# Half of the second feed-forward product of an encoder layer by a seven-product block scheme on whole 512-column halves

## The chip, the cores and the metric

The kernel runs on one core of one Trainium2 chip. The metric is the device time of one execution in microseconds (us); less is better. The engines are TensorE (PE in the profile, PEld for its weight loads), VectorE (DVE), ScalarE (ACT), GpSimd (POOL) and SyncE (SP), the last of which here only issues transfers.

## The reference, cut to what matters

One layer of an encoder on `x` of 512 tokens by 1024 features, float32. The change touches the last product and the norm behind it:

```
n2 = rms_norm(h, norm_mlp_pre)                                   # 512 x 1024
hid = square(relu(einsum('bsd,df->bsf', n2, w_up)))              # 512 x 4096
mlp_out = einsum('bsf,fd->bsd', hid, w_down)                     # 512 x 1024, over f = 4096
h = h + rms_norm(mlp_out, norm_mlp_post)
```

## The kernel before, in words

Every large product is made in float32 precision out of three matmuls on rounded halves. An operand `a` is split into `hi` (ScalarE copies it into the type `F32R`, line 79) and `lo` (VectorE subtracts `hi` from `a`, line 80); the helper is `split_into`, and `split_back` (line 888) is the same with its result in a tile of the pool `wback`, tag `hl`, five buffers. `mm3` (lines 82 to 86) then adds `ah*bh + ah*bl + al*bh` into one bank of PSUM: three matmuls, lines 84, 85 and 86.

The order of the instructions on each engine is fixed when the program is built, by the planner of the tile framework: it goes through a modelled time, and among the instructions whose inputs and buffers are there by then, the one written first goes first. `tc.issue_after(ins)` puts what is written in its block behind `ins` on the same engine. A pool with N buffers for a tag hands out the next tile only when an earlier one is no longer read.

The first feed-forward product (`up`, lines 969 to 1003) leaves 32 tiles of `hid`, each 128 features by 512 tokens, in four tiles of eight (`hida` three, `hidb` one). Most of it is already made by a seven-product scheme on 256-column blocks (`product`, line 961).

The second product (`down`, lines 1005 to 1053) sums over those 32 feature tiles f into eight PSUM banks `accs[t][hf]`: t is the block of 128 tokens (0 to 3), hf the half of 512 output columns (0 or 1). The loop over `f2` (line 1018) loads two row blocks of `w_down` at once (1 MB, tile `dnw`, tag `raw`, two buffers, queue of SP, line 1020). For each of the two f it splits the weights (`split_back`, 128x1024) and the hidden tile (`split_into`, 128x512), and calls `down` for the eight banks: 24 matmuls of 128x512 columns for each f, 768 in all. The matmuls of the last four f (`NLAST`) are kept back and done bank by bank, so that the norm behind one block of tokens (`post_norm`, lines 805 to 813) can run beside the matmuls of the next. That norm squares a half on ScalarE with a running sum (line 808), weighs it by the gain on VectorE (line 811), takes the power -0.5 on GpSimd (line 96) and adds the residual on VectorE (line 813); then the block goes out in two transfers (line 1050).

Of the kernel before, what the change touches and what calls it, by code (L numbers as in the profile page):

```python
# [10 lines left out]
F32 = mybir.dt.float32  # L11
F32R = mybir.dt.float32r
AF = mybir.ActivationFunctionType
ALU = mybir.AluOpType
PSUM = bass.MemoryType.PSUM

P = 128
S = 512
D = 1024
KD = D // P  # L20
FF = 4096
KF = FF // P
# [14 lines left out]
def block_kernel(ctx: ExitStack, tc: tile.TileContext, x, norm_mix_pre, w_in, b_gate, ln_v_gain, ln_v_bias,  # L37
                 w_spatial, b_spatial, w_branch_a, w_branch_b, w_out, norm_mix_post, norm_mlp_pre, w_up,
                 w_down, norm_mlp_post, ident_c, rope_c, mask_c, perm_c, out):
    nc = tc.nc  # L40
    x, out, w_in, w_up, w_down, w_out = x[0], out[0], w_in[0], w_up[0], w_down[0], w_out[0]
    w_branch_a, w_branch_b, w_spatial = w_branch_a[0], w_branch_b[0], w_spatial[0]

    def pool(stack, name, bufs=1, space=None, side=None):
        kw = {"side": side} if side else {}
        if space is not None:
            kw["space"] = space
        return stack.enter_context(tc.tile_pool(name=name, bufs=bufs, reuse_waits="tile", **kw))

    consts = pool(ctx, "consts")  # L50
    small = pool(ctx, "small", bufs=4)
# [26 lines left out]
    def split_into(hi, lo, src, sub=nc.vector):  # L78
        nc.scalar.activation(hi, src, AF.Copy)  # L79
        return sub.tensor_tensor(lo, src, hi.bitcast(F32), op=ALU.subtract)  # L80

    def mm3(ps, a, b, start, stop):
        (ah, al), (bh, bl) = a, b
        nc.tensor.matmul(ps, ah, bh, start=start, stop=False)  # L84
        nc.tensor.matmul(ps, ah, bl, start=False, stop=False)  # L85
        return nc.tensor.matmul(ps, al, bh, start=False, stop=stop)  # L86

    def rstd_of(ss, mult, eps=EPS):
        t = small.tile([P, 1], F32, name="rs_in")
        nc.vector.tensor_scalar(t, ss[:, 0:1], mult, eps, op0=ALU.mult, op1=ALU.add)  # L90
        if ss.shape[1] == 2:
            t2 = small.tile([P, 1], F32, name="rs_in2")
            nc.vector.scalar_tensor_tensor(t2, ss[:, 1:2], mult, t, op0=ALU.mult, op1=ALU.add)
            t = t2
        r = small.tile([P, 1], F32, name="rs_out")
        nc.gpsimd.tensor_tensor(r, t, neghalf[:, :1], op=ALU.pow)
        return r
# [6 lines left out]
    right = ExitStack()  # L104
# [20 lines left out]
    start = ExitStack()  # L125
# [91 lines left out]
    for i in range(4):  # L217
        if i + 1 < 4:
            _, hi, lo = norm_x(blocks[i + 1], xts[i + 1], rs[i + 1])
# [4 lines left out]
        b = blocks[i]  # L224
# [4 lines left out]
        t = vtmp.tile([P, 2, GW], F32R, name="v0", bufs=2)  # L229
# [89 lines left out]
    for i, (vec, n) in enumerate(((b_gate, 16), (ln_v_gain, 4), (ln_v_bias, 4), (norm_mlp_pre, 8))):  # L319
        o = (0, 16, 20, 24)[i]  # L320
# [364 lines left out]
    for g2 in range(2):  # L685
        raw = wload([KD, 2 * P], lambda r: [(r, fcols(w_in, COL_U + g2 * 2 * P, KD, 2 * P))], "uw")
        for j in range(2):
            g = 2 * g2 + j
            wh, wl = wsplit(raw[:, :, j * P:(j + 1) * P], sub=nc.gpsimd)
            ps = psA.tile([P, S], F32, name="pf", tag="acc" if g else "T", bufs=4 if g else 1)  # L690
# [14 lines left out]
            t = gpool.tile([P, 4, P], F32, name="sv")  # L705
# [59 lines left out]
    for d in range(GSTD):  # L765
        g2 = gate_rows(d - GSTD)
        raw = gate_raw(d)
        for br in range(2):
            ps = feature_tile(*wsplit(raw[:, :, 1 - br]), KD, nhn, nln)
# [8 lines left out]
    back = ExitStack()  # L778
    psB = pool(back, "psB", space=PSUM)
    spacer(back, 224, "nedge")  # L780
    n2pool = pool(back, "n2pool", bufs=8, side="right")
# [6 lines left out]
    gain = hpool.tile([P, D], F32, name="gain", bufs=1)  # L788
    nc.gpsimd.dma_start(gain, norm_mix_post.to_broadcast([P, D]))
    h2d = tc.dram_tile([S, D], F32, name="h2d")  # L790
    halves = [slice(0, 512), slice(512, 1024)]
# [10 lines left out]
    def all_banks():  # L802
        return [[psB.tile([P, 512], F32, name="pd", tag=tg, bufs=4) for _ in range(2)] for tg in ("tp", "tp", "acc", "acc")]

    def post_norm(pss, gain, ys, dst, res, junk):
        ss = small.tile([P, 2], F32, name="ss2")
        for hf, hs in enumerate(halves):
            nc.scalar.activation(junk[hf], pss[hf].rearrange("p (k c) -> p k c", c=P), AF.Square, accum_out=ss[:, hf:hf + 1])
            if hf:
                r = rstd_of(ss, 1.0 / D)  # L810
            nc.vector.tensor_tensor(ys[hf], pss[hf], gain[:, hs], op=ALU.mult)
        for hf, hs in enumerate(halves):
            nc.vector.scalar_tensor_tensor(dst[:, hs], ys[hf], r, res[:, hs], op0=ALU.mult, op1=ALU.add)
# [38 lines left out]
    for t in range(4):  # L852
# [18 lines left out]
        r = rstd_of(ss, 1.0 / D)  # L871
# [16 lines left out]
    def split_back(src, shape):  # L888
        hl = wback.tile([P, 2] + shape, F32R, name="hl", tag="hl")
        split_into(hl[:, 0], hl[:, 1], src)  # L890
        return hl[:, 0], hl[:, 1]

    hida = pool(back, "hida", bufs=3)
    dn = ExitStack()
    d0pool = pool(dn, "d0pool", bufs=2)
    up = ExitStack()
    upool = pool(up, "upool", bufs=2)
    hid = []
# [1 line left out]
    def hid_of(f):  # L900
        return hid[f // 8][:, f % 8]
# [100 lines left out]
    tail()  # L1002
    up.close()

    dpool = pool(dn, "dpool", bufs=2)
    NLAST = 4
    lpool = pool(dn, "lpool", bufs=1)
    epool = pool(dn, "epool", bufs=NLAST)
    gain = n2pool.tile([P, D], F32, name="gain3", tag="n2")
    nc.gpsimd.dma_start(gain, norm_mlp_post.to_broadcast([P, D]))  # L1010
    accs = all_banks()

    def down(t, f, hf, hh, hl, wh, wl):
        ts_ = slice(t * P, (t + 1) * P)
        mm3(accs[t][hf], (hh[:, ts_], hl[:, ts_]), (wh[:, halves[hf]], wl[:, halves[hf]]), f == 0, f == KF - 1)

    last = []
    for f2 in range(KF // 2):
        raw = wback.tile([P, 2, D], F32, name="dnw", tag="raw", bufs=2)
        nc.sync.dma_start(raw, w_down[f2 * 2 * P:(f2 + 1) * 2 * P].rearrange("(k p) c -> p k c", p=P))  # L1020
        for j in range(2):
            f = 2 * f2 + j
            end = f >= KF - NLAST
            wh, wl = split_back(raw[:, j], [D])
            if end:
                hhl = epool.tile([P, 2, S], F32R, name="hhl")
                hh, hl = hhl[:, 0], hhl[:, 1]
            else:
                dp = dpool if f > 1 else d0pool
                hh = dp.tile([P, S], F32R, name="hh")  # L1030
                hl = dp.tile([P, S], F32R, name="hl")
            with tc.issue_after(late[0].ins), tc.issue_after(late[1].ins):
                split_into(hh, hl, hid_of(f))
            if end:
                last.append((f, hh, hl, wh, wl))
            else:
                for t in range(4):
                    for hf in range(2):
                        down(t, f, hf, hh, hl, wh, wl)
    for t in range(4):  # L1040
        ts_ = slice(t * P, (t + 1) * P)
        h2 = n2pool.tile([P, D], F32, name="h2", tag="n2")
        nc.gpsimd.dma_start(h2, h2d[ts_])
        for hf in range(2):
            for f, hh, hl, wh, wl in last:
                down(t, f, hf, hh, hl, wh, wl)
        o = lpool.tile([P, D], F32, name="o", bufs=2)
        post_norm(accs[t], gain, [lpool.tile([P, 512], F32, name="y", bufs=2) for _ in range(2)], o, h2, [o[:, hs].rearrange("p (k c) -> p k c", c=P) for hs in halves])
        for hs in halves:
            nc.sync.dma_start(out[t * P:(t + 1) * P, hs], o[:, hs])  # L1050
    dn.close()
    back.close()

# [40 lines left out]
```

## Time and profile before

| | us |
|---|---|
| time of the runs: median of 3 (lowest, highest) | 808.02 (807.9, 809.44) |
| span of the profiled execution, first to last instruction | 806.0 |
| its own time | not listed apart from the three runs; the median lies 2.0 above its span |
| PE busy in the span | 793.4 (98%) |
| DVE busy | 540.0 (67%) |
| ACT busy | 422.1 (52%) |
| POOL busy | 59.7 (7%) |

How to read the profile: a row of a group gives the source line (which can be a helper's), the engine, the operation, the tiles written and read with their shapes, the number of instructions, their busy time together and the mean length of one, and then the idle time of the engine in front of them with what ended it. A row of the timeline gives the start, the length, the engine, the line, the operation and the tiles. Matmuls overlap in the pipe, so that the length of one is more than the distance between two; distances between starts are used here.

### The profile page before, as it was taken

The page shows a single profiled execution, that of the slowest core. Times are in us where ns is not written, and L with a number is a line of the kernel's source. Part 1 is how long each engine was busy: PE and PEld are TensorE (multiplying, and loading weights), DVE is VectorE, ACT ScalarE, POOL GpSimd, SP SyncE. Part 2 cuts the span into 40 slices and gives each one's busy share as a digit, 9 for nine tenths or more (in the row PEclk, how much of TensorE's full clock was granted, in tenths as well). Part 3 has the DMA queues.
Part 4 walks back from the last instruction along what each step waited for, and adds up shares of the span by engine and source line. Part 5 has one row for each costly group of instructions (what it writes and reads, how often), then busy time and mean ns, then how long its engine had stood idle before and what let it go on. Part 6 is the DMA issues. An engine that isn't in the chain of part 4 may idle for free.

```text
span 806.0 us, 12336 instructions
## 1 busy us (share of the span) xinstructions
PE 793.4 (98%) x4917; PEld 718.9 (89%) x4917; DVE 540.0 (67%) x915; ACT 422.1 (52%) x721; POOL 59.7 (7%) x86
## 2 busy tenths in 40 slices
PE   9999999999999999999999999999999999999996
PEld 6899999998988889999988899999999888888885
DVE  6784688978655877887655489988896633333324
ACT  6351477878576464554445457666666532332212
POOL 3300100010104300000001102000000000000000
PEclk9999999999999999999999999999999999999999
DMA  9643733343625424353446123333334533332202
GB/s 321 220 119 106 202 94 105 105 132 105 185 74 123 130 79 106 102 134 79 158 159 223 62 79 105 106 106 115 108 114 159 211 105 105 104 105 86 72 1 105
DMA packets 90603, 98.92 MB, mean 123 GB/s; under 512 B 2689, under 2 KB 74401, under 8 KB 90546
## 3 DMA queue, kind: packets, MB, share of 16 engines
q1 hardware_dynamic: 80208, 77.60, 31.5%
q0 software_dynamic: 10336, 20.54, 8.3%
q8 instruction: 38, 0.62, 0.3%
q14 instruction: 19, 0.16, 0.1%
q10 hardware_dynamic: 2, 0.00, 0.0%
HBM read 88.17 MB, written 9.96 MB: 122 GB/s over the span
## 4 chain that ended last, share of the span: by engine, by line
PE 94%; DVE 3%; ACT 2%; issue 0%; DMA 0%; DVEq 0%; POOLq 0%; POOL 0%; ACTq 0%
PE pacc L961 12%; PE pg L343 9%; PE pd L84 9%; PE pd L85 9%; PE pd L86 9%; PE pgacc L343 6%; PE pf L84 5%; PE pf L85 5%; PE pf L86 5%; PE ptp L961 5%; PE pv L85 4%; PE pv L84 4%; PE pv L86 4%; PE pgS L343 2%; PE psb L498 1%; PE py L617 1%
## 5 line engine op out<-in xcount | busy, mean ns | idle before, releaser
L85 PE MATMUL pd<-hl,hh 128*128 128x512 f32 x224 | 87.2, 389 | 0.0
L84 PE MATMUL pd<-hl,hh 128*128 128x512 f32 x224 | 86.5, 389 | 0.0
L86 PE MATMUL pd<-hl 128*128 128x512 f32 x224 | 86.0, 389 | 0.0
L80 DVE TENSOR_TENSOR hl<-hid,hh 128x512 fp32r<-128x512 f32 x28 | 19.2, 693 | 75.6 <-ACT hh L79 75.6
L961 PE MATMUL pacc<-nt,hl 128*128 128x256 f32 x504 | 66.9, 279 | 1.4 <-DVE nt L80 1.4
L79 ACT ACTIVATE hh<-hid 128x512 fp32r<-128x512 f32 x28 | 17.4, 630 | 89.0 <-PE pd L85 89.0
L961 PEld LDWEIGHTS pacc<-nt,hl 128*128 128x128 f32 x504 | 62.3, 188 | 1.6 <-DVE nt L80 1.6
L85 PEld LDWEIGHTS pd<-hl,hh 128*128 128x128 f32 x224 | 42.0, 188 | 8.7
L86 PEld LDWEIGHTS pd<-hl 128*128 128x128 f32 x224 | 42.0, 188 | 8.7
L84 PEld LDWEIGHTS pd<-hl,hh 128*128 128x128 f32 x224 | 42.0, 188 | 8.7
L80 DVE TENSOR_TENSOR hl<-dnw,hl 128x1024 fp32r<-128x1024 f32 x32 | 39.1, 1226 | 14.5 <-ACT hl L79 14.5
L961 PE MATMUL pacc<-n,hl 128*128 128x256 f32 x336 | 44.9, 279 | 0.0
L84 PE MATMUL pf<-nh,hi 128*128 128x512 f32 x112 | 44.6, 398 | 0.0
L74 ACT ACTIVATE hi<-s 128x1024 fp32r<-128x1024 f32 x30 | 31.7, 1059 | 23.9 <-DVE s L330 10.5
L85 PE MATMUL pf<-nl,hi 128*128 128x512 f32 x112 | 43.9, 392 | 0.0
L86 PE MATMUL pf<-nh,lo 128*128 128x512 f32 x112 | 43.9, 392 | 0.0
L79 ACT ACTIVATE hl<-s 128x1024 fp32r<-128x1024 f32 x28 | 29.6, 1057 | 27.1 <-DVE s L945 17.6
L75 DVE TENSOR_TENSOR lo<-s,hi 128x1024 fp32r<-128x1024 f32 x30 | 36.6, 1224 | 9.7 <-ACT hi L74 9.6
L961 PEld LDWEIGHTS pacc<-n,hl 128*128 128x128 f32 x336 | 41.8, 188 | 0.1
L79 ACT ACTIVATE hl<-dnw 128x1024 fp32r<-128x1024 f32 x32 | 33.4, 1048 | 13.1 <-PE pacc L961 7.9
L80 DVE TENSOR_TENSOR hl<-s,hl 128x1024 fp32r<-128x1024 f32 x28 | 34.2, 1221 | 6.6 <-ACT hl L79 6.6
L85 PE MATMUL pv<-lo,nh 128*128 128x512 f32 x96 | 38.2, 397 | 0.0
(361 smaller groups left out, 2227.3 us busy)
## 6 DMA issues: line engine op xcount, KB each, us to landing
upw<-in_w_up_dram SPq DMA_DIRECT2D x16, 1024.0 KB, 5.5
dnw<-in_w_down_dram SPq DMA_DIRECT2D x16, 1024.0 KB, 4.9
qkw<-in_w_in_dram SPq DMA_DIRECT2D x24, 512.0 KB, 5.3
gw<-in_w_in_dram SPq DMA_DIRECT2D x16, 512.0 KB, 5.4
slab<-in_w_in_dram SPq DMA_DIRECT2D x6, 1024.0 KB, 9.4
wow<-in_w_out_dram SPq DMA_DIRECT2D x4, 1024.0 KB, 4.9
w0raw<-in_w_in_dram SPq DMA_DIRECT2D x4, 512.0 KB, 7.0
v0d<-v POOLq DMA_DIRECT2D x4, 512.0 KB, 4.7
```

Source lines behind the costliest of these rows:

```text
L74: nc.scalar.activation(hi, raw, AF.Copy)
L75: (sub or nc.vector).tensor_tensor(lo, raw, hi.bitcast(F32), op=ALU.subtract)
L79: nc.scalar.activation(hi, src, AF.Copy)
L80: return sub.tensor_tensor(lo, src, hi.bitcast(F32), op=ALU.subtract)
L84: nc.tensor.matmul(ps, ah, bh, start=start, stop=False)
L85: nc.tensor.matmul(ps, ah, bl, start=False, stop=False)
L86: return nc.tensor.matmul(ps, al, bh, start=False, stop=stop)
L343: nc.tensor.matmul(ps, a[:, j], b[:, j], start=first and not (j or i), stop=(j == KH - 1 and i == 2), skip_group_check=True)
L498: nc.tensor.matmul(ps[:, rr, g - 1], got["q", g][:, r], got["k", g][:, r], start=True, stop=True)
L617: nc.tensor.matmul(o, v12[:, g, r], ptb[r // 2][:, r % 2, g], start=False, stop=(r == 3 and g == 1), skip_group_check=True)
L961: nc.tensor.matmul(ps, a[:, j], b[:, j], start=first and not (j or m), stop=(j == KH - 1 and m == 2), skip_group_check=True)
```

## The change

Of the 32 feature tiles, f = 0 to 15 stay as they were (`plain`, two f at a time, f2 = 0 to 7). The other sixteen are taken as a 2x2 block product: the hidden operand A in blocks of tokens (rows 0 to 255 and 256 to 511) by the parity of f, the weights B in blocks of the parity of f by the column half. Each block of B is eight row blocks of 128 by 512 columns, handled in two chunks c = 0 and 1 of four. Instead of eight block products of 48 matmuls there are seven of 48, on sums of blocks:

- S3 = A11-A21, S2 = A22-S3, S1 = A11+S2, S4 = A12-S2, made in place in `hid` and in two tiles `s2`;
- T3 = B22-B12, then T2 = T3+B11, T1 = B22-T2, and B21-T2, made in `tsum` (and `t1`);
- P7 = S3*T3 and P6 = S2*T2 and A22*(B21-T2) are added into the two banks Y (tokens 256 to 511, half 0), P1 = A11*B11 and P2 = A12*B21 into X (tokens 0 to 255, half 0), P5 = S1*T1 into Z (tokens 256 to 511, half 1), P3 = S4*B22 into W (tokens 0 to 255, half 1).

The products go into the same eight banks that hold the sums of the plain part. Copies of the banks at certain times (`p1`, `r22`, `r12`, `z0`, in a tile `keep`) let the parts be taken apart again: P1 = X after minus X before, and so on. The order written is: plain 0 to 2; first sums for c = 0; plain 3; first sums for c = 1; plain 4 (banks in the order `y_first`); copies of Y and X; P7; copy of Y; P1 and P6 in alternating pieces of twelve matmuls; `p1` and `v`; plain 5 to 7 (`z_first`); copy of Z; P5 and P3 in alternating pieces; the sums that finish half 1, with its part of the norm (`weigh`); then the last two products into Y and X, the second chunk bank by bank, each bank followed by `finish`.

Blocks of weights are loaded as tiles of 128 x 4 x 512 through the same two `raw` buffers: B22, B12, B11, B22 again and B21, each in two chunks, so ten loads of 1 MB for the seven-product half. The hidden tiles are split two f at a time (128x1024) into a tile `hhl`, tag `hhl`: one buffer for the first, three for the others. The weights' splits stay in the five `hl` buffers. The pool `epool` and the kept-back last four f go.

```diff
@@ -892,7 +892,7 @@
 
     hida = pool(back, "hida", bufs=3)
     dn = ExitStack()
-    d0pool = pool(dn, "d0pool", bufs=2)
+    d0pool = pool(dn, "d0pool", bufs=1)
     up = ExitStack()
     upool = pool(up, "upool", bufs=2)
     hid = []
@@ -1002,52 +1002,187 @@
     tail()
     up.close()
 
-    dpool = pool(dn, "dpool", bufs=2)
-    NLAST = 4
-    lpool = pool(dn, "lpool", bufs=1)
-    epool = pool(dn, "epool", bufs=NLAST)
+    dpool = pool(dn, "dpool", bufs=3)
+    lpool = pool(dn, "lpool", bufs=2)
+    sumpool = pool(back, "sumpool", side="right")
     gain = n2pool.tile([P, D], F32, name="gain3", tag="n2")
     nc.gpsimd.dma_start(gain, norm_mlp_post.to_broadcast([P, D]))
     accs = all_banks()
-
-    def down(t, f, hf, hh, hl, wh, wl):
-        ts_ = slice(t * P, (t + 1) * P)
-        mm3(accs[t][hf], (hh[:, ts_], hl[:, ts_]), (wh[:, halves[hf]], wl[:, halves[hf]]), f == 0, f == KF - 1)
-
-    last = []
-    for f2 in range(KF // 2):
-        raw = wback.tile([P, 2, D], F32, name="dnw", tag="raw", bufs=2)
-        nc.sync.dma_start(raw, w_down[f2 * 2 * P:(f2 + 1) * 2 * P].rearrange("(k p) c -> p k c", p=P))
+    X, W, Y, Z = [[accs[t][hf] for t in ts] for ts, hf in (((0, 1), 0), ((0, 1), 1), ((2, 3), 0), ((2, 3), 1))]
+    N7 = 8
+    F7 = KF - 2 * N7
+    FA = 10
+    tsl = [slice(t * P, (t + 1) * P) for t in range(4)]
+
+    def raw_down():
+        return wback.tile([P, 2, D], F32, name="dnw", tag="raw", bufs=2)
+
+    def hid_split(first, src, shape):
+        hl = (d0pool if first else dpool).tile([P, 2] + shape, F32R, name="hhl", tag="hhl")
+        with tc.issue_after(late[0].ins), tc.issue_after(late[1].ins):
+            split_into(hl[:, 0], hl[:, 1], src)
+        return hl[:, 0], hl[:, 1]
+
+    def acc3(ps, a, b, start, stop):
+        (ah, al), (bh, bl) = a, b
+        nc.tensor.matmul(ps, ah, bh, start=start, stop=False, skip_group_check=True)
+        nc.tensor.matmul(ps, ah, bl, start=False, stop=False, skip_group_check=True)
+        return nc.tensor.matmul(ps, al, bh, start=False, stop=stop, skip_group_check=True)
+
+    def plain(f2, order):
+        f = 2 * f2
+        raw = raw_down()
+        nc.sync.dma_start(raw, w_down[f * P:(f + 2) * P].rearrange("(k p) c -> p k c", p=P))
+        hh, hl = hid_split(not f, hid[f // 8][:, f % 8:f % 8 + 2], [2, S])
         for j in range(2):
-            f = 2 * f2 + j
-            end = f >= KF - NLAST
             wh, wl = split_back(raw[:, j], [D])
-            if end:
-                hhl = epool.tile([P, 2, S], F32R, name="hhl")
-                hh, hl = hhl[:, 0], hhl[:, 1]
+            for t, hf in order:
+                acc3(accs[t][hf], (hh[:, j, tsl[t]], hl[:, j, tsl[t]]), (wh[:, halves[hf]], wl[:, halves[hf]]),
+                     f + j == 0, f + j in (FA - 1, F7 - 1))
+
+    w7 = w_down[F7 * P:].rearrange("(c j h p) d -> c h p j d", p=P, h=2, j=4)
+
+    def block(c, h, hf):
+        raw = raw_down()
+        raw = raw.rearrange("p a (b d) -> p (a b) d", d=512)
+        nc.sync.dma_start(raw, w7[c, h, :, :, halves[hf]])
+        return raw
+
+    def w_split(src):
+        return [split_back(src[:, 2 * i:2 * i + 2], [2, 512]) for i in range(2)]
+
+    def h_split(src):
+        return hid_split(False, src, [4, 256])
+
+    def chunk(ps, h, w, stop):
+        for i in range(2):
+            piece(ps, h, w, i, stop and i == 1)
+
+    def piece(ps, h, w, i, stop=False):
+        (hh, hl), (wh, wl) = h, w[i]
+        for j in range(2):
+            for t in range(2):
+                acc3(ps[t], (hh[:, 2 * i + j, tsl[t]], hl[:, 2 * i + j, tsl[t]]), (wh[:, j], wl[:, j]), False, stop and j == 1)
+
+    order = [(t, hf) for t in range(4) for hf in range(2)]
+    y_first = [(2, 0), (3, 0), (0, 0), (1, 0), (0, 1), (1, 1), (2, 1), (3, 1)]
+    for f2 in range(3):
+        plain(f2, order)
+    blk = [hid[F7 // 8 + c].rearrange("p (j h) s -> p j h s", h=2) for c in range(2)]
+    a11, a12, a21, a22 = [[b[:, :, h, z * 256:z * 256 + 256] for b in blk] for z in range(2) for h in range(2)]
+    tsum = sumpool.tile([P, N7, 512], F32, name="tsum")
+    tsum = [tsum[:, 4 * c:4 * c + 4] for c in range(2)]
+    s2 = []
+
+    def two(out, x, y, op):
+        for i in range(0, 4, 2):
+            nc.vector.tensor_tensor(out[:, i:i + 2], x[:, i:i + 2], y[:, i:i + 2], op=op)
+
+    def first_sums(c):
+        b22, b12 = block(c, 1, 1), block(c, 0, 1)
+        two(tsum[c], b22, b12, ALU.subtract)
+        nc.vector.tensor_tensor(a21[c], a11[c], a21[c], op=ALU.subtract)
+        s2.append(n2pool.tile([P, 4, 256], F32, name="s2", tag="n2"))
+        nc.vector.tensor_tensor(s2[c], a22[c], a21[c], op=ALU.subtract)
+
+    first_sums(0)
+    plain(3, order)
+    first_sums(1)
+    plain(4, y_first)
+    keep = hida.tile([P, 8, S], F32, name="hid")
+    p1, r22, r12, z0 = [keep[:, 2 * i:2 * i + 2] for i in range(4)]
+    for dst, src in ((r22, Y), (p1, X)):
+        for i in range(2):
+            nc.scalar.activation(dst[:, i], src[i], AF.Copy)
+
+    for c in range(2):
+        chunk(Y, h_split(a21[c]), w_split(tsum[c]), c == 1)
+    for i in range(2):
+        nc.scalar.activation(r12[:, i], Y[i], AF.Copy)
+    for c in range(2):
+        b11 = block(c, 0, 0)
+        h, w = h_split(a11[c]), w_split(b11)
+        two(tsum[c], tsum[c], b11, ALU.add)
+        h6, w6 = h_split(s2[c]), w_split(tsum[c])
+        nc.vector.tensor_tensor(a11[c], a11[c], s2[c], op=ALU.add)
+        nc.vector.tensor_tensor(s2[c], a12[c], s2[c], op=ALU.subtract)
+        for i in range(2):
+            piece(X, h, w, i, c == 1 and i == 1)
+            piece(Y, h6, w6, i, c == 1 and i == 1)
+    for i in range(2):
+        nc.vector.tensor_tensor(p1[:, i], X[i], p1[:, i], op=ALU.subtract)
+    v = n2pool.tile([P, 2, 512], F32, name="v", tag="n2")
+    for i in range(2):
+        nc.vector.tensor_tensor(v[:, i], Y[i], p1[:, i], op=ALU.add)
+
+    z_first = [(2, 1), (3, 1), (0, 1), (1, 1), (0, 0), (1, 0), (2, 0), (3, 0)]
+    for f2 in range(FA // 2, F7 // 2):
+        plain(f2, z_first)
+    for i in range(2):
+        nc.scalar.activation(z0[:, i], Z[i], AF.Copy)
+    nc.vector.tensor_tensor(r22, v, r22, op=ALU.subtract)
+    nc.vector.tensor_tensor(r12, v, r12, op=ALU.subtract)
+    nc.vector.tensor_tensor(r12, r12, z0, op=ALU.subtract)
+
+    for c in range(2):
+        b22 = block(c, 1, 1)
+        h, w = h_split(s2[c]), w_split(b22)
+        h5, w5 = h_split(a11[c]), []
+        for i in range(2):
+            t1 = n2pool.tile([P, 2, 512], F32, name="t1", tag="n2")
+            nc.vector.tensor_tensor(t1, b22[:, 2 * i:2 * i + 2], tsum[c][:, 2 * i:2 * i + 2], op=ALU.subtract)
+            w5.append(split_back(t1, [2, 512]))
+        for i in range(2):
+            piece(Z, h5, w5, i, c == 1 and i == 1)
+            piece(W, h, w, i, c == 1 and i == 1)
+
+    def finish(t, srcs, ys, o, ss):
+        h2 = n2pool.tile([P, D], F32, name="h2", tag="n2")
+        nc.gpsimd.dma_start(h2, h2d[tsl[t]])
+        for hf in (1, 0):
+            if srcs[hf] is not None:
+                if ys[hf] is None:
+                    ys[hf] = lpool.tile([P, 512], F32, name="y")
+                weigh(srcs[hf], ys[hf], o[:, halves[hf]], ss, hf)
+        r = rstd_of(ss, 1.0 / D)
+        for hf, hs in enumerate(halves):
+            nc.vector.scalar_tensor_tensor(o[:, hs], ys[hf], r, h2[:, hs], op0=ALU.mult, op1=ALU.add)
+        for hs in halves:
+            nc.sync.dma_start(out[tsl[t], hs], o[:, hs])
+
+    def weigh(src, y, junk, ss, hf):
+        nc.scalar.activation(junk, src, AF.Square, accum_out=ss[:, 1 - hf:2 - hf])
+        nc.vector.tensor_tensor(y, src, gain[:, halves[hf]], op=ALU.mult)
+
+    sums = [small.tile([P, 2], F32, name="ss2") for _ in range(4)]
+    for i in range(2):
+        nc.vector.tensor_tensor(r12[:, i], W[i], r12[:, i], op=ALU.add)
+        nc.vector.tensor_tensor(r12[:, i], Z[i], r12[:, i], op=ALU.add)
+        nc.vector.tensor_tensor(r22[:, i], Z[i], r22[:, i], op=ALU.add)
+        weigh(r12[:, i], r12[:, i], z0[:, i], sums[i], 1)
+        weigh(r22[:, i], r22[:, i], v[:, i], sums[2 + i], 1)
+
+    for c in range(2):
+        b21 = block(c, 1, 0)
+        two(tsum[c], b21, tsum[c], ALU.subtract)
+        h4, w4 = h_split(a22[c]), w_split(tsum[c])
+        h, w = h_split(a12[c]), w_split(b21)
+        if c:
+            break
+        for i in range(2):
+            piece(Y, h4, w4, i)
+            piece(X, h, w, i)
+    for ps, (hh, hl), ws, ts in ((Y, h4, w4, (2, 3)), (X, h, w, (0, 1))):
+        for t in range(2):
+            for j in range(4):
+                wh, wl = ws[j // 2]
+                acc3(ps[t], (hh[:, j, tsl[t]], hl[:, j, tsl[t]]), (wh[:, j % 2], wl[:, j % 2]), False, j == 3)
+            o = lpool.tile([P, D], F32, name="o")
+            if ps is Y:
+                nc.vector.tensor_tensor(p1[:, t], Y[t], p1[:, t], op=ALU.add)
+                finish(2 + t, [p1[:, t], None], [p1[:, t], r22[:, t]], o, sums[2 + t])
             else:
-                dp = dpool if f > 1 else d0pool
-                hh = dp.tile([P, S], F32R, name="hh")
-                hl = dp.tile([P, S], F32R, name="hl")
-            with tc.issue_after(late[0].ins), tc.issue_after(late[1].ins):
-                split_into(hh, hl, hid_of(f))
-            if end:
-                last.append((f, hh, hl, wh, wl))
-            else:
-                for t in range(4):
-                    for hf in range(2):
-                        down(t, f, hf, hh, hl, wh, wl)
-    for t in range(4):
-        ts_ = slice(t * P, (t + 1) * P)
-        h2 = n2pool.tile([P, D], F32, name="h2", tag="n2")
-        nc.gpsimd.dma_start(h2, h2d[ts_])
-        for hf in range(2):
-            for f, hh, hl, wh, wl in last:
-                down(t, f, hf, hh, hl, wh, wl)
-        o = lpool.tile([P, D], F32, name="o", bufs=2)
-        post_norm(accs[t], gain, [lpool.tile([P, 512], F32, name="y", bufs=2) for _ in range(2)], o, h2, [o[:, hs].rearrange("p (k c) -> p k c", c=P) for hs in halves])
-        for hs in halves:
-            nc.sync.dma_start(out[t * P:(t + 1) * P, hs], o[:, hs])
+                finish(t, [X[t], None], [None, r12[:, t]], o, sums[t])
     dn.close()
     back.close()
```

## The prediction

> **What bounds the kernel now.** I read the page first, then the chain, the stages, the waits, and last the timeline of the second product.
>
> ```profile
> PE 793.4 (98%) x4917; PEld 718.9 (89%) x4917; DVE 540.0 (67%) x915; ACT 422.1 (52%) x721; POOL 59.7 (7%) x86
> PE 94%; DVE 3%; ACT 2%; issue 0%; DMA 0%; DVEq 0%; POOLq 0%; POOL 0%; ACTq 0%
> 640.00:780.00 140.00, 140.00 (x619) 115.95 (x618) 49.11 (x52) 39.25 (x50) 0.00 (x0) 1.00 0.27 91
> PE pacc L961 <- DVE nt L80: 1.4, 1, 1.4
> ```
>
> TensorE is busy 98% of the span, and the chain that ends last runs through it for 94%. The third row is the heart of the second product (columns: stretch, length, busy us and count of PE, PEld, DVE, ACT, POOL, granted clock, share and GB/s of the transfers): PE has no gap in 140 us, at full clock, while DVE works 35% and ACT 28%. The last row is PE's longest wait anywhere, 1.4 us. So here time is the number of matmuls times their distance, plus a tail.
>
> ```profile
> 641.57 0.39 PE L84 MATMUL pd<-hl,hh 128*128 128x512 f32 x1
> 647.01 0.39 PE L84 MATMUL pd<-hl,hh 128*128 128x512 f32 x1
> 798.65 0.39 PE L84 MATMUL pd<-hl,hhl 128*128 128x512 f32 x1
> 799.11 0.39 PE L86 MATMUL pd<-hl,hhl 128*128 128x512 f32 x1
> ```
>
> The first two rows begin f = 3 and f = 4: 24 matmuls in 5.44 us, 0.227 us each. The last two lie in the final run of twelve into one bank, two steps in 0.46 us: the order of the banks does not change the distance.
>
> **The change part by part: matmuls.** 768 become 16 x 24 + 7 x 48 = 720. All are 128x512 with 128 stationary columns, as before, so 48 x 0.227 = **10.9 us** leave the path, if PE stays fed. The rest asks whether it does.
>
> **Splits and sums.** The durations, and the distances where two follow each other:
>
> ```profile
> L80 DVE TENSOR_TENSOR hl<-dnw,hl 128x1024 fp32r<-128x1024 f32 x32 | 39.1, 1226 | 14.5 <-ACT hl L79 14.5
> L79 ACT ACTIVATE hl<-dnw 128x1024 fp32r<-128x1024 f32 x32 | 33.4, 1048 | 13.1 <-PE pacc L961 7.9
> 637.18 1.99 ACT L79 ACTIVATE hl<-dnw 128x1024 fp32r<-128x1024 f32 x2
> 638.25 2.36 DVE L80 TENSOR_TENSOR hl<-dnw,hl 128x1024 fp32r<-128x1024 f32 x2 [0.96 <-ACT hl L79]
> ```
>
> A split of 128x1024 is 1.05 on ACT, then 1.23 on DVE: 2.3 us from free buffer to usable tile; queued, they follow at 1.0 and 1.18. A sum of two blocks of 128x1024 is one more DVE unit of that size (I take the same price; SBUF operands of the same type and size). Units of DVE per stage, with PE's time for that stage: a `plain`, 3 units (3.5 us) in 10.9; first sums, 4 for each c; P7, 6 (7.1) in 10.9; P1 with P6, 20 (23.6) in 21.8; P5 with P3, 16 (18.9) in 21.8; the last two products, 16 (18.9) in 21.8, with ten operations on 128x512 for half 1 (L811's 0.69 below, queued about 0.62, so 6.2) and the norms. With three more for `r22` and `r12` that is 93 units over the whole second product, 110 us, and some 20 us on half widths, in 163 us of matmuls: DVE is not the bound on average. It exceeds PE in P1 with P6, but there PE's own buffers hold work ahead: five `hl` tiles, each worth twelve matmuls (2.7 us) in these stages, are prepared up to 10.9 us early, and P7 before it leaves 3.8 us of DVE free. I cost this stage at nothing; without the early buffers it would cost 23.6 - 21.8 = 1.8 us. ACT, with about 2 units for each piece of twelve where DVE has 2 to 2.5, is never the tighter.
>
> **Copies and banks.** Y is copied on ACT before P7 may add to it. In `y_first`, Y's last matmul stands 18 matmuls (4.1 us) ahead of P7's first; the two copies, of the size of L808's 0.60 us below, fit. After P7 the two copies `r12` have the first piece of P1 (2.7 us) to hide in. X is read for `p1`, Y for `v`, with 2.7 and 4.1 us of other banks' matmuls before their next use. All at nothing, by that cover; uncovered, about 1.3 us each.
>
> **The loads in plain 3 and 4.** This is where I expect a cost. The two `raw` buffers serve B22 and B12 together, since T3 needs both; only after the subtraction is either free. So four loads stand in a row: B12 (c = 0), plain 3, B12 (c = 1), plain 4, each waiting for what is made of the one before.
>
> ```profile
> dnw<-in_w_down_dram SPq DMA_DIRECT2D x16, 1024.0 KB, 4.9
> upw<-in_w_up_dram SPq DMA_DIRECT2D x16, 1024.0 KB, 5.5
> slab<-in_w_in_dram SPq DMA_DIRECT2D x6, 1024.0 KB, 9.4
> w0raw<-in_w_in_dram SPq DMA_DIRECT2D x4, 512.0 KB, 7.0
> 630.43 0.37 SPq L1020 DMA_DIRECT2D dnw<-in_w_down_dram  x1
> 639.50 0.37 SPq L1020 DMA_DIRECT2D dnw<-in_w_down_dram  x1
> 635.18 1.14 ACT L79 ACTIVATE hhl<-hid 128x512 fp32r<-128x512 f32 x2
> ```
>
> Before, the fourth and fifth loads go out at 630.43 and 639.50, the latter when the splits of the third are done (the DVE row at 638.25: 1.23 later). After, those two are B22 and B12 of c = 0, at the same times, since all that leads up to them is the same. From there, with 4.9 us a load: B12 there at 644.4; two subtractions, 646.8; plain 3's load there at 651.7, both halves split by 655.2; B12 of c = 1 there at 660.1; subtracted, 662.5; plain 4's load there at 667.4; first half split, 669.7 (hi at 668.5). PE wants it at the start of f = 8: 641.57 + 5 x 5.44 = 668.8, and the second matmul, at 669.0, already wants lo. That is a gap of 0.7 us; with the two loads of B12 landing 0.3 later each (their rows of 2 KB lie between `dnw`'s 4 KB and the 1 KB of `upw`, 5.5 us) and a hand-over of 0.1 at each of eight steps, 2.1. I take **1.8**. Plain 3 has 3 us of slack (wanted at 641.57 + 3 x 5.44 = 657.9, its first half there at 654.0). The bounds: nothing, if the splits of the third load come 2 us earlier; above, see the next point and the rival on loads.
>
> The second cost is order. T3 of c = 1 is ready 4.9 us before plain 4's weights land, and the planner gives free buffers to what is ready: in the last row above ACT splits hidden tiles of the kept-back f (28 up), long ahead of their use. If the two splits of T3 take the two free `hl` tiles at 662.5, plain 4's second half waits until its own first half has been multiplied: another 2.3 us of split, and 0.5 on the first. So between 0 and 2.9 us. I take **1.5**, the middle, since the order in modelled time cannot be read from this trace.
>
> **The last two stages.** From the start of P5 to the end lie 43.5 us of matmuls and 2.7 of tail. DVE has there 32 units less the 8 that the buffers allow ahead, 24 x 1.18 = 28.3, the 6.2 of half 1, and four `finish` (2.3 to 3.0 each), about 10: 44.5 of 46.2 us. It just fits. Each piece frees its `hl` tile 2.7 us before the tile made in it is next wanted in the tightest place (`h5` of c = 1, in the third `hhl` buffer), and a split takes 2.3. I take **0.5** lost, between 0 and what the rival below gives.
>
> **The tail.**
>
> ```profile
> 799.53 0.60 ACT L808 ACTIVATE o<-pd 128x512 f32<-128x512 f32 x1 [1.98 <-PE pd L86]
> 800.33 0.69 DVE L811 TENSOR_TENSOR y<-pd,gain 128x512 f32<-128x512 f32 x1
> 801.14 1.42 DVE L813 SCALAR_TENSOR_TENSOR o<-y,rs_out,h 128x512 f32<-128x512 f32 x2
> ```
>
> Before: last square at 799.53, results at 802.56, then the transfer. After, the same chain, except that banks end every 2.7 us instead of pairs every 5.4, so DVE may still be at the block before (3.0 us of `finish` for each of tokens 256 to 511): **0.3**, between 0 and 0.7.
>
> **Sum.** -10.9 + 1.8 + 1.5 + 0.5 + 0.3 = **-6.8 us**: the span goes from 806.0 to 799.2, the time from 808.02 to **801.2**, with the same 2.0 us around the span as between the profiled execution and the median of the runs.
>
> **The rivals.**
> (a) The loads and the order fit: no gap in plain 4. Then 808.0 - 10.9 + 0.3 = 797.4. For it: before, PE waits for no `dnw` at all in this product. Against: the sum of the four loads above.
> (b) DVE becomes the bound of the last 43 us. Every split lets DVE wait a little for ACT:
>
> ```profile
> 703.00 1.22 DVE L80 TENSOR_TENSOR hl<-dnw,hl 128x1024 fp32r<-128x1024 f32 x1 [0.26 <-ACT hl L79]
> ```
>
> Sixteen splits of 0.26 are 4.2 us on top of 44.5, 2.5 over the 46.2; with an order of the queue that serves half 1's sums first, 4. Time 801.2 + 4 = 805. For it: the narrow fit; against: a free DVE elsewhere lets the planner move sums forward.
> (c) The load chain is longer, and the kernel becomes slower: each us more per load costs 4 in the gap of plain 4. At w0raw's 7.0 us (half the size, at the crowded start) the gap is 1.8 + 4 x 2.1 = 10.2 and the gain is gone; that is the point where it decides. At slab's 9.4 it is 19.8, and the time some 816. For it: 2 MB more to load and pairs of loads in flight; against: the stage above moves 91 GB/s with the transfer engines 27% busy, so a load that is 4.9 us there has little to meet.
> (d) The gap costs clock besides. At the start, matmuls of this size stood 0.43 us apart:
>
> ```profile
> 9.43 0.63 PE L85 MATMUL pv<-w0lo,nh 128*128 128x512 f32 x1
> 9.86 0.63 PE L86 MATMUL pv<-w0hi,nl 128*128 128x512 f32 x1
> ```
>
> If a wait in plain 4 brings that back for ten matmuls, 10 x 0.20 = 2 us: 803.2. The Trainium skill ("TensorE: Matmul & The Clock Gate", section "HAM oscillation — how this bites in real kernels") asks for no idle gap of TensorE above about 3.4 us, lest the clock fall back; before has no such gap, so no run here shows it, and by that rule my two gaps, of about 2 us each, are each too short for it.
> (e) That the saving is not there, because matmuls into alternating banks or on tiles of four are farther apart: the rows at 798 to 799 speak against it. About 808.
>
> **How the numbers follow.** Forecast with its gaps 0.45, range of its own 798.5 to 803.5; (a) 0.22; (b) 0.17; (c) 0.09; (d) 0.05; (e) 0.02. Faster by over 0.2% (1.6 us, about what a measurement of this kernel can tell from no change) are the forecast, (a), (d) and most of (b): 0.87. Same: (e) and a corner of (b) and (c), 0.05. Slower: the rest of (c), 0.08. For the range 797.0 to 806.0, I leave out (c), (e), the lower edge of (a) and the upper of (b), together 0.2.
>
> **What would show it.** 4869 matmuls instead of 4917; 18 loads `dnw` of 1 MB instead of 16; distance still 0.227. A wait of PE for DVE (`lo` of weights) at the first matmul of plain 4's weights, near 669, and perhaps one 5.4 us later; none in plain 0 to 3, P7, P1 with P6, plain 5 to 7. DVE nearly full over the last 45 us, and about 600 us busy in all. I am wrong if the gap in plain 4 is above 6 us, if PE waits more than 2 us in the last two stages, or if the tail from the last matmul to the end, now 7 us, grows by more than 1.

## The result, and the profile after

The changed kernel takes 802.99 us (median of four runs, 802.89 to 803.42) against 808.52 (807.9 to 809.44): a ratio of 0.9932, 95% interval 0.9918 to 0.9946. That is 5.5 us less; 6.8 were forecast. The profiled execution took 802.89 with a span of 801.1, 4.9 less than before's 806.0; the balance below is that of the spans.

The page after, its waits of TensorE (us in total, times, longest), and two stretches of the second product (columns as in the prediction):

```profile
PE 782.8 (98%) x4869; PEld 709.8 (89%) x4869; DVE 593.8 (74%) x956; ACT 442.1 (55%) x731; POOL 60.2 (8%) x86
PE 87%; DVE 5%; DMA 3%; ACT 3%; issue 1%; POOL 0%; DVEq 0%; POOLq 0%; ACTq 0%
PE pd L1028 <- ACT hl L79: 1.4, 1, 1.4
PE pacc L961 <- DVE nt L80: 1.4, 1, 1.4
681.30:790.40 109.10, 109.09 (x482) 90.00 (x480) 85.06 (x90) 51.79 (x61) 3.78 (x6) 1.00 0.25 89
768.30:790.40 22.10, 22.09 (x98) 17.97 (x96) 20.32 (x32) 11.24 (x20) 1.61 (x2) 1.00 0.03 12
```

The 48 matmuls are gone. TensorE has one new wait, of 1.4 us, and from P7 to the last matmul none at all, although VectorE is 92% busy in the 22 us up to there. But the chain that ended last now has 5% on VectorE and 3% on transfers, where before had 3% and none. That points to the end of the kernel. The timeline of the end:

```profile
790.01 0.39 PE L1030 MATMUL pd<-hl,hhl 128*128 128x512 f32 x1
788.08 2.74 DVE L1149 SCALAR_TENSOR_TENSOR o<-hid,rs_out,h 128x512 f32<-128x512 f32 x4 [0.39 <-POOL rs_out L96]
791.72 0.60 ACT L1154 ACTIVATE o<-pd 128x512 f32<-128x512 f32 x1 [4.82 <-DMA out_dram<-o]
793.07 0.60 ACT L1154 ACTIVATE o<-pd 128x512 f32<-128x512 f32 x1 [0.66 <-DMA out_dram<-o]
797.41 0.75 DVE L1149 SCALAR_TENSOR_TENSOR o<-hid,rs_out,h 128x512 f32<-128x512 f32 x1
```

The last matmul ends at 790.40, 9.1 us sooner than before's 799.50. From there to the last result before took 3.06 us; this takes 7.76, to 798.16. ScalarE stands idle for 4.82 us in front of the square of bank X0, and an output transfer ends that wait. About 2.4 of the 4.82 are due to the transfer: the bank itself is complete only 1.1 us before the last matmul's end (the first variant below shows it). The square's unused output is written into a tile `o`; there are two, and the first is still on its way out with tokens 256 to 383, whose last step (the first half of the row at 788.08) came just before. The balance: 9.1 gained, 4.7 lost in the tail, 0.5 gained behind the last result, 4.9 in the span.

### The profile page after: what moved, and what is told of

Same layout as the page of the kernel before. It is cut to its first block, busy times and chain, and to the rows that moved or that the text cites. A ratio compares the mean times of both kernels' runs of the same rounds, so it can differ in the third digit from the quotient of the medians.

```text
span 801.1 us, 12250 instructions
## 1 busy us (share of the span) xinstructions
PE 782.8 (98%) x4869; PEld 709.8 (89%) x4869; DVE 593.8 (74%) x956; ACT 442.1 (55%) x731; POOL 60.2 (8%) x86
## 4 chain that ended last, share of the span: by engine, by line
PE 87%; DVE 5%; DMA 3%; ACT 3%; issue 1%; POOL 0%; DVEq 0%; POOLq 0%; ACTq 0%
PE pacc L961 12%; PE pg L343 9%; PE pgacc L343 6%; PE pd L1028 5%; PE pf L84 5%; PE pd L1029 5%; PE pd L1030 5%; PE pf L85 5%; PE pf L86 5%; PE ptp L961 5%; PE pv L85 4%; PE pv L86 4%; PE pv L84 4%; PE pgS L343 3%; DMA dnw<-in_w_down_dram 2%; PE pd L84 2%
## 5 line engine op out<-in xcount | busy, mean ns | idle before, releaser
L1029 PE MATMUL pd<-hl,hhl 128*128 128x512 f32 x240 | 93.3, 389 | 0.0
L1030 PE MATMUL pd<-hl,hhl 128*128 128x512 f32 x240 | 91.3, 389 | 0.0
L1028 PE MATMUL pd<-hl,hhl 128*128 128x512 f32 x240 | 88.7, 390 | 1.4 <-ACT hl L79 1.4
L1028 PEld LDWEIGHTS pd<-hl,hhl 128*128 128x128 f32 x240 | 45.0, 188 | 11.1 <-ACT hl L79 1.9
L1030 PEld LDWEIGHTS pd<-hl,hhl 128*128 128x128 f32 x240 | 45.1, 188 | 9.3
L1029 PEld LDWEIGHTS pd<-hl,hhl 128*128 128x128 f32 x240 | 45.1, 188 | 9.3
L79 ACT ACTIVATE hl<-dnw 128x1024 fp32r<-128x1024 f32 x28 | 29.3, 1055 | 40.6 <-PE pd L1030 17.1
L80 DVE TENSOR_TENSOR hl<-dnw,hl 128x1024 fp32r<-128x1024 f32 x28 | 33.9, 1221 | 15.9 <-ACT hl L79 15.9
L86 PE MATMUL pv<-hi,nl 128*128 128x512 f32 x96 | 37.8, 397 | 0.0
L84 PE MATMUL pv<-hi,nh 128*128 128x512 f32 x96 | 37.1, 395 | 0.0
```

What stands on the lines that cost most here:

```text
L1028: nc.tensor.matmul(ps, ah, bh, start=start, stop=False, skip_group_check=True)
L1029: nc.tensor.matmul(ps, ah, bl, start=False, stop=False, skip_group_check=True)
L1030: return nc.tensor.matmul(ps, al, bh, start=False, stop=stop, skip_group_check=True)
```

## Experiments

Single executions of some variants lie up to 3 us apart, as much as the effects sought. So beside the medians I compare positions within the profiled executions: TensorE's wait in plain 4, and the time from the last matmul's end to the last result ("tail").

**Four output tiles.**

```diff
-            o = lpool.tile([P, D], F32, name="o")
+            o = lpool.tile([P, D], F32, name="o") if ps is Y else n2pool.tile([P, D], F32, name="o", tag="n2")
```

> The two output tiles of tokens 0 to 255 come from two free buffers of another pool, so the four tiles `o` share nothing. Theory A (output buffers): the changed kernel's tail of 10.7 us, from the last matmul's end at 790.4 to 801.1, is long because the squares of the X banks write into an `o` tile whose transfer out has still to land (waits of 4.8 and 0.7 us of ScalarE for `out_dram`). Without that wait X0's square starts about 788.0, not 791.7, and the last results are ready 3 to 5 us sooner: time 798.0 to 800.0, against 802.99. Theory B (VectorE is behind at the end): four `finish` at 2.7 us distance are too many for VectorE, whichever tile they write; the tail shortens by less than 1 us: time 802 to 803.

```profile
790.68 0.39 PE L1030 MATMUL pd<-hl,hhl 128*128 128x512 f32 x1
789.97 0.60 ACT L1154 ACTIVATE o<-pd 128x512 f32<-128x512 f32 x1 [2.40 <-PE pd L1030]
791.10 0.60 ACT L1154 ACTIVATE o<-pd 128x512 f32<-128x512 f32 x1 [0.44 <-PE pd L1030]
794.84 0.74 DVE L1149 SCALAR_TENSOR_TENSOR o<-hid,rs_out,h 128x512 f32<-128x512 f32 x1
```

Median 801.29 (800.84 to 803.03; before, on the same chip, 807.98), ratio 0.9922 (0.9909 to 0.9934). The squares now wait for the matmuls alone, and the tail is 795.58 - 791.07 = 4.51 us instead of 7.76: 3.25 gained, as theory A has it for the tail. The time misses its 798 to 800: TensorE came to its last matmul 0.7 us later in this execution, 0.4 of it in plain 4's wait (1.9 us here), and the median carries the spread. The rows show something else: the squares of X0 and X1 start 1.13 us apart, five matmuls instead of twelve (2.7 us). So the planner had mixed the matmuls of the last banks, where theory A's 788.0 for X0's square took the written order, and two norms end up together at the end.

This variant also pays something that "tail" leaves out. From the last result to the end of the span it takes 3.9 us, where the change takes 3.0:

```profile
789.20 0.58 POOL L1141 DMA_DIRECT2D h<-h2d  x1
DMA to landing us min/median/max: 3.0/3.0/4.5
```

The second row is of the output transfers; in the change they land after 2.0 to 2.1 us. The pool that lends the two extra tiles also holds the residual `h2`, and here one of its loads (512 KB) goes out only at 789.20, beside the output. That this load is what slows them is likely, but no run isolates it. The two fastest versions below have the same late load.

**Only the squares' unused output elsewhere.**

```diff
-                weigh(srcs[hf], ys[hf], o[:, halves[hf]], ss, hf)
+                weigh(srcs[hf], ys[hf], junk, ss, hf)
```

Here `junk` is `v[:, t]` for Y and `z0[:, t]` for X, which are free by then.

> Only the squares' unused output goes elsewhere (into `z0` and `v`, which are free by then); the results still go into two `o` tiles. Theory A, in its strict form that only the squares' target matters: as with four tiles, 798.0 to 800.0. Theory A, in the form that the buffer counts for the results too: X0's and X1's squares start at once, but the results of X0 wait for the first transfers to land at 791.7 and those of X1 for about 793.1, ready at 794.6 where 798.2 was; a gain of 3 to 3.6 us, time 799.4 to 800.0, no better than four tiles and up to 1 us worse. Theory B: less than 1 us, 802 to 803.

Median 802.18 (799.9 to 803.05), ratio 0.9921 (0.9909 to 0.9934); the tail is 4.17 us, no longer than with four tiles, and without the late load it takes 3.0 us from the last result to the end of the span.

```profile
792.16 0.39 PE L1030 MATMUL pd<-hl,hhl 128*128 128x512 f32 x1
795.97 0.75 DVE L1149 SCALAR_TENSOR_TENSOR o<-hid,rs_out,h 128x512 f32<-128x512 f32 x1
```

So the strict form holds: what cost 3 us was the square's unused output in `o`, not the room for the results, which VectorE comes to only when the transfers have landed. The median says little; in the profiled execution TensorE ended 2.1 us later than in the changed kernel, of which 0.3 in plain 4's wait and the rest in earlier stages that this edit does not touch (the last section has the larger part of it).

**The first sums one plain earlier.**

```diff
-    for f2 in range(3):
+    for f2 in range(2):
         plain(f2, order)
...
     first_sums(0)
+    plain(2, order)
     plain(3, order)
```

> The first sums for c = 0, with their two loads, stand before plain 2 instead of behind it. Chain theory (loads of B12, plain 3, B12 and plain 4 stand in a row): the row starts one plain (10.9 us) sooner, plain 2 joins it with one load and its splits (about 7 us), and plain 4's weights are there some 3 us sooner than the 670.4 at which TensorE now starts on them; its wait of 1.44 us goes, time 801.5 plus or minus 0.3. Rival (the wait comes from the order of splits on ScalarE, not from the loads): the wait stays between 1 and 2 us, time 802.7 to 803.3.

The wait in plain 4 is gone, TensorE has none left in this product, and the last matmul ends at 788.85, 1.55 us sooner than in the change. Median 802.42 (801.19 to 802.62), ratio 0.9926 (0.9912 to 0.9939); the profiled execution took 801.38. The place agrees with the chain theory; the median misses its 801.2 to 801.8 and agrees only in its sign.

**One more load in the row.**

```diff
         two(tsum[c], b22, b12, ALU.subtract)
+        if c:
+            two(tsum[c], block(c, 1, 1), b12, ALU.subtract)
```

> For c = 1, T3 is made twice, with B22 loaded again in between: one more load (4.9 us) and two more subtractions (2.4 us) in the row of loads ahead of plain 4, and 3 us of VectorE elsewhere free. Chain theory: the wait at plain 4 grows by 7.3 us, from 1.44 to 8.7; time 802.99 + 7.3 = 810.3 if TensorE goes on at its full distance of 0.227 us after it. If a gap of that length costs clock (the Trainium skill, TensorE: Matmul & The Clock Gate, section HAM oscillation, names about 3.4 us as the gap that does), the matmuls behind it stand 0.43 us apart for a few us: 1.5 to 2 us more, about 812, and the granted clock of that stretch is below 1. Rival (the wait has nothing to do with the row of loads): time below 805.

```profile
PE pd L1028 <- ACT hl L79: 9.3, 1, 9.3
678.42:684.00 5.58, 5.58 (x14) 4.39 (x15) 5.58 (x5) 3.73 (x4) 0.00 (x0) 0.53 0.53 179
682.00 0.63 PE L1029 MATMUL pd<-hl,hhl 128*128 128x512 f32 x1
682.43 0.63 PE L1030 MATMUL pd<-hl,hhl 128*128 128x512 f32 x1
683.69 0.40 PE L1029 MATMUL pd<-hl,hhl 128*128 128x512 f32 x1
```

The wait grows from 1.44 to 9.34 us, by 7.9 where 7.3 were worked out. Behind it the granted clock is 0.53, and twelve matmuls (678.42 to 683.69) take 5.3 us where they take 2.7. The last matmul comes 10.4 us later (7.9 + 2.5); the time, of a single execution, is 814.23. So the mechanism of rival (d) exists. The Trainium skill ("TensorE: Matmul & The Clock Gate", section "HAM oscillation — how this bites in real kernels") has it for gaps above about 3.4 us, and this run agrees; the next variant shows that a shorter gap can do it too. In the change's profile the granted clock stayed at 1.00 behind the 1.4 us.

**The last banks and their norms in turn.**

```diff
+            with tc.issue_after(done.ins) if done else nullcontext():
                 for j in range(4):
...
+            with tc.issue_after(norm.ins) if norm else nullcontext():
                 if ps is Y:
```

Here `done` is the last matmul of the bank before, `norm` the last VectorE instruction of its `finish`.

> The changed kernel with the last four banks forced into the written order: each bank's twelve matmuls behind the last of the bank before, and each bank's norm behind the one before on VectorE and ScalarE. The planner had mixed them: X0 and X1 end 1.13 us apart, Y1 only 5 us before the end. Two output tiles as in the change. Theory C (the mixed order is the main cause of the long tail): from the last matmul's end to the last result 3.1 to 3.8 us instead of 7.8; time about 799. Theory A (the two output tiles are the main cause, the order a smaller one): the first block's results are ready some 2.7 us sooner, but the squares of X still wait for transfers that have to land; 5 to 6.5 us, time 800.5 to 801.5.

Median 803.40 (803.16 to 805.15), ratio 0.9938 (0.9924 to 0.9951), the tail 7.4 us. Both theories missed. The profiled execution, the slowest of the five at 805.15, shows the clock as well:

```profile
671.41 2.56 PE L1028 MATMUL pd<-hl,hhl 128*128 128x512 f32 x8 [2.18 <-ACT hl L79]
673.77 0.63 PE L1029 MATMUL pd<-hl,hhl 128*128 128x512 f32 x1
674.19 0.63 PE L1030 MATMUL pd<-hl,hhl 128*128 128x512 f32 x1
676.31 0.39 PE L1029 MATMUL pd<-hl,hhl 128*128 128x512 f32 x1
671.40:680.00 8.60, 8.59 (x31) 6.92 (x32) 8.60 (x8) 5.75 (x6) 0.00 (x0) 0.80 0.44 155
```

Here a wait of only 2.18 us in plain 4 is followed by a granted clock of 0.80 over 8.6 us, with matmuls 0.43 us apart; by the starts up to 676.31, fourteen matmuls took 4.9 us where they take 3.2, so 1.7 were lost. So the 3.4 us that the Trainium skill names in that section are no safe bound here; the measurement decides.

The same order together with four tiles and the early sums:

> All three together: four output tiles, the first sums for c = 0 ahead of plain 2, the last four banks in the written order. If the three causes are the whole of what the change lost, TensorE has no wait in the second product, its last matmul ends 10.6 to 10.9 us sooner than before's 799.5, so 788.6 to 789.3 with what the earlier stages vary, and the tail from there to the last result is 3.1 to 3.5 us as before's 3.1; time 797.2 to 798.2, ratio 0.987 to 0.988. If something else is lost besides (clock in the tail, a transfer), the time stays above 799.

Median 801.35 (800.92 to 801.85), ratio 0.9914 (0.99 to 0.9927). TensorE has no wait, as expected, and ends at 789.68, 0.4 us past the expected range, but the tail is again 7.4 us, with four tiles:

```profile
789.29 0.39 PE L1030 MATMUL pd<-hl,hhl 128*128 128x512 f32 x1
790.21 0.19 ACT L1156 ACTIVATION_READ_ACCUMULATOR o<-pd 128x1 f32 x1
794.04 0.68 DVE L1157 TENSOR_TENSOR y<-pd,gain 128x512 f32<-128x512 f32 x1
795.64 0.75 DVE L1150 SCALAR_TENSOR_TENSOR o<-y,rs_out,h 128x512 f32<-128x512 f32 x1 [0.66 <-POOL rs_out L96]
796.31 0.75 DVE L1150 SCALAR_TENSOR_TENSOR o<-hid,rs_out,h 128x512 f32<-128x512 f32 x1
```

The last square is done at 790.4, its bank is weighed at 794.04. VectorE was kept in the norm before, and inside each norm it waits for ScalarE's sum and GpSimd's power (0.66 in the row): one norm after another takes 4.3 us for a Y bank and 2.9 for an X bank, 14.4 for four that used to overlap. My own order made the third cause. Two runs tell it apart, both with four tiles and the early sums: the first without any order by hand, the second with the matmuls in turn (`done`) and VectorE free:

> Four output tiles and the first sums for c = 0 ahead of plain 2; nothing ordered by hand in the last banks. From the two runs that did each alone: no wait of TensorE in the second product, last matmul's end at 788.9 to 789.3, and the tail of the run with four tiles, 4.5 us to the last result. Time 798 to 799.5. If the gains do not add (the planner chooses another order), above 800.

Median 798.94 (798.71 to 799.01), ratio 0.9888 (0.9872 to 0.9905): no wait of TensorE, its end at 788.79, a tail of 4.5 us. The two gains add.

> As the kernel with four output tiles and early first sums, and the twelve matmuls of each of the last four banks in turn, but VectorE's order left to the planner. Theory D (in the run with all three, the tail of 7.4 us came from putting each bank's norm wholly behind the one before on VectorE, which then waits for ScalarE and GpSimd inside each norm, some 4.3 us for each of Y and 2.9 for each of X): without that chain the norms overlap, and the last result is ready 3.5 to 4.2 us after the last matmul; time 797.2 to 798.5. Rival (the banks in turn are themselves what lengthens the tail): it stays at 6 us or more, time above 800.

```profile
786.08 2.74 DVE L1150 SCALAR_TENSOR_TENSOR o<-hid,rs_out,h 128x512 f32<-128x512 f32 x4 [0.39 <-POOL rs_out L96]
786.66 0.19 ACT L1155 ACTIVATION_READ_ACCUMULATOR o<-pd 128x1 f32 x1
788.46 0.39 PE L1030 MATMUL pd<-hl,hhl 128*128 128x512 f32 x1
788.74 0.69 DVE L1156 TENSOR_TENSOR y<-pd,gain 128x512 f32<-128x512 f32 x1
789.61 0.69 DVE L1156 TENSOR_TENSOR y<-pd,gain 128x512 f32<-128x512 f32 x1
792.27 0.75 DVE L1150 SCALAR_TENSOR_TENSOR o<-hid,rs_out,h 128x512 f32<-128x512 f32 x1
```

Median 798.46 (798.18 to 798.73) against 807.91, ratio 0.9883 (0.9868 to 0.9898): theory D. The tail is 793.02 - 788.85 = 4.17 us. This is the fastest version, 9.5 us below before; its interval lies wholly below that of the change (0.9918 to 0.9946). What the mixed order of banks costs by itself is small, 0.3 us of tail, and the 0.5 us between the two medians is no more than their intervals allow.

The tail is still 1.1 us longer than before's 3.06. X0's square is done at 786.85, but VectorE is busy with the block before until 788.8 and comes to the bank at 788.74. That is what the forecast had in mind for the tail; no run isolates it. And this version and the one before it have the late load of `h2`: 3.70 and 3.85 us from the last result to the end, against 3.0. By these figures they would gain an estimated 0.7 to 0.9 us with the squares' output elsewhere (as in the second variant) in place of four tiles; that was not run.

## Where the prediction was right and where it was not, point by point

- **Matmuls, -10.9.** Right. Without the wait, TensorE ends at 788.85, 10.65 before; the first feed-forward product alone ended 0.2 to 0.45 us later in these executions (VectorE's row 632.68 of the change against 632.23).
- **Loads in plain 4, 1.8.** Right in place and cause, near in size: 1.44. Two errors met. The row of loads starts 2.0 us later than I had it, at 641.47 instead of 639.50. About 1.2 of that is ScalarE's: it comes to plain 2's last split at 638.39 instead of 637.18, behind hidden tiles that are now split at twice the width and a first product that ended up to 0.45 later. The other 0.8 come from the planner, which put S3's subtraction ahead of that split's second step on VectorE:

```profile
638.39 1.05 ACT L79 ACTIVATE hl<-dnw 128x1024 fp32r<-128x1024 f32 x1
639.09 1.22 DVE L1084 TENSOR_TENSOR hid<-hid 128x1024 f32<-128x1024 f32 x1
640.22 1.22 DVE L80 TENSOR_TENSOR hl<-dnw,hl 128x1024 fp32r<-128x1024 f32 x1
641.47 0.37 SPq L1048 DMA_DIRECT2D dnw<-in_w_down_dram  x1
664.43 0.37 SPq L1035 DMA_DIRECT2D dnw<-in_w_down_dram  x1
669.27 2.00 ACT L79 ACTIVATE hl<-dnw 128x1024 fp32r<-128x1024 f32 x2 [10.12 <-DMA dnw<-in_w_down_dram]
670.38 2.14 PE L1028 MATMUL pd<-hl,hhl 128*128 128x512 f32 x8 [1.44 <-ACT hl L79]
671.18 1.99 ACT L79 ACTIVATE hl<-tsum 128x1024 fp32r<-128x1024 f32 x2
```

   And TensorE did not need `lo` at its second matmul: the planner put the eight matmuls that read only `hi` first (x8 in the row at 670.38), which cover VectorE's 1.2 us. So it waited for ScalarE's `hi`, and not for VectorE's `lo` as I had it.
- **Order of the splits, 1.5.** Wrong: nothing. The row at 669.27 holds both of plain 4's splits; those of T3 follow at 671.18, although T3 had been there since 664.4. The planner did not give the buffers away.
- **VectorE in the last two stages, 0.5, and rival (b).** Nothing was lost on TensorE. Over the last 43.6 us of matmuls VectorE was busy 34.8, and 39.5 up to the last result, where I had 44.5: less was left for it than I had counted. The last 22 us, at 20.3, are the narrow part, and the buffers held.
- **The tail, 0.3.** This is the term that failed: it was 4.7 in the tail, 4.2 net of what came back behind the last result. My own sign of being wrong, a growth of more than 1 us from the last matmul to the end, came true: 6.5 became 10.7. I saw that banks would end every 2.7 us instead of pairs every 5.4, and asked only what that does to VectorE. I did not ask what the two `o` tiles, which had 5.4 us between uses, do at half that distance, with a result, a transfer of 2.1 us and a square that writes to `o` ahead of everything. The runs give that square's output 3.3 to 3.6 of the 4.7 (the tails of the first two variants, 4.51 and 4.17); about 0.3 is the mixed order of the banks, and the rest most likely VectorE at the block before, the one cause that I had named. I also took the written bank order for the order of the program.
- The terms that cost nothing (1.5 + 0.5) and the tail (4.4 too little) offset each other in part: -4.9 in the span where -6.8 was forecast. So the time lies in the range partly by luck: two errors have opposite signs. Rivals (a), (c) and (e) are ruled out by the profile after: there is a gap, it is short, and the 48 matmuls are saved in full. Rival (d), which I held to need a longer gap, did not occur in that profile, but did behind a gap of 2.18 us in a variant, so that 0.05 was a low chance for it. The 816 us of rival (c) leave out the other losses of the sum; with them it is 819, and nothing hung on it.

## What to carry to other kernels

When a change halves the distance between the ends of banks, go through every buffer and every wait of the epilogue at the new distance, unused outputs of accumulating instructions included: a scratch write into a tile that is leaving cost over 3 us here, more than twice the one stall that came of those that were feared (1.4). Before taking more tiles for it, look at what else lives in the pool that lends them. Where a planner fixes the order, an order by hand needs a measurement of its own: with the matmuls of the banks in turn the tail was 0.3 us shorter, with whole norms in turn it was 3 us longer. A load that must meet another before either buffer is free makes a row of loads; moving its start by one step took the wait away, and no run shows a cost of it.

## What was not expected of the hardware

In two profiles a wait of TensorE cost clock behind it: 2.5 us after 9.3 us of waiting, and 1.7 us after 2.18. Waits of 1.4, 1.8 and 1.9 us in other profiles left the granted clock at 1.00.

Executions of some variants that keep plain 4's wait differ by up to 3 us (with four output tiles alone 800.84 to 803.03, in two groups 1.7 apart), while the two fastest versions, which have no such wait, stay within 0.6 (798.71 to 799.01, 798.18 to 798.73). A clock lost in some executions and not in others would give that, but the early-sums variant, without the wait, also spread by 1.4. The mean clocks listed for the executions do not settle it, because the clock also falls behind the last matmul, where it costs nothing: in the change's profile 0.61 over the last 10.7 us alone make its mean of 0.995. And there is another source of spread, in the first feed-forward product, which no variant touches; the same stretch in the change's profile and in that of the second variant:

```profile
490.00:610.00 120.00, 118.57 (x1016) 118.36 (x1016) 106.43 (x151) 77.23 (x110) 2.42 (x1) 1.00 0.34 107
490.00:610.00 120.00, 118.57 (x1006) 118.37 (x1006) 105.63 (x149) 76.52 (x109) 3.11 (x1) 1.00 0.35 109
```

At the same granted clock of 1.00 TensorE gets through ten matmuls fewer in 120 us, about 1.1 us of work. The variant with all three edits together has 1007 there, the other eight profiles 1016 or 1017. Why is not known. Which executions lost clock, and which lost time here, only a profile of each would tell, so the spread stays open.
